# A memset ahead of the second of three loads in a 180-degree rotation

## The chip, the cores and the metric

The kernel runs on one core of one Trainium2 chip. The metric is device time in microseconds (us), taken from whole executions; the times before are the median of three. A profile is one more execution, recorded by the hardware profiler; its span goes from the first to the last instruction, so it is a little shorter than the device time. A core has five instruction queues that matter here by name: VectorE (DVE in the profile) does the copies, SyncE (SP) and ScalarE (ACT) issue transfers, GpSimd (POOL) sets four constants at the start, TensorE (PE) has no work. Transfers between the main memory (HBM) and the on-chip memory (SBUF, 128 partitions) run on 16 DMA engines, which all queues share.

## The reference

```python
def setup_inputs():
    batch, c, h, w = 32, 3, 256, 256
    return {"x": np.random.randn(batch, c, h, w).astype(np.float32)}

def reference(x: np.ndarray) -> np.ndarray:
    return np.rot90(x, k=2, axes=(-2, -1)).astype(np.float32)
```

Each of the 96 images of 256 x 256 numbers is turned by 180 degrees. As an image lies row after row, this is the same as writing its 65,536 numbers in reverse order. Nothing is calculated: 25.17 MB are read and 25.17 MB are written.

## The kernel before

The 96 images are cut into three groups of 32. In a group every image is cut into four quarters of E = 16384 numbers, so that a group fills a tile of 128 partitions (32 images x 4 quarters) with 16384 columns of float32: 64 KB a partition, 8.39 MB a tile. There are three such tiles, one for each group: `A`, `Bt` (called Bt in the profile, B by its tag) and `Ct`. A fourth, `T`, has J = 2048 columns and holds what is set aside in a swap. No tile is used twice for different groups, so the loads wait for nothing.

To reverse an image, the numbers inside each quarter are reversed by VectorE in the tile, and the four quarters of an image change places when the tile is stored: the output's access pattern has `::-1` over the four.

- `load` (line 54) issues one transfer for a whole tile. SyncE issues the loads of `A` and `Ct` (lines 69 and 71), ScalarE that of `Bt` (line 70). This is all that ScalarE does.
- `swap` (line 61) exchanges one block of columns at the front with its mirror block at the back, both reversed, by three copies on VectorE: the back block reversed into `T`, the front block reversed into the back, `T` into the front. `copy` (line 52) keeps these copies in the order of the program.
- `turn` (line 73) does this for a range of the front half in blocks of at most 2048 columns.
- `store` (line 57) issues one transfer from a tile to the output, on SyncE.

The order on VectorE is written out by hand: three blocks of `A`, a first piece of `Bt` (MID = 1008 columns), the last block of `A`, the rest of `Bt`, then `Ct`: 39 copies in all. SyncE issues, after its two loads, a first store of `A` (LEAD = 256 columns), the rest of `A`, then `Bt` and `Ct`, each when VectorE is done with it. Semaphore waits are put in by the framework from which instruction writes and which reads a tile: a load waits for an earlier instruction that writes the same columns, a copy for the load of its tile, a store for the copies.

Of the kernel before, what the change touches and what calls it, by code (L numbers as in the profile page):

```python
# [2 lines left out]

os.environ.setdefault("NEURON_RT_ULTRASERVER_MODE", "4")

# [4 lines left out]


@with_exitstack
def kernel(
    ctx: ExitStack,
    tc: tile.TileContext,
    x: bass.AP,
    out: bass.AP,
):

    nc = tc.nc
    P = 128

    B, C, H, W = x.shape
    L = H * W
    G = 32
    E = L // 4
    J = E // 8

    x4 = x.rearrange("b c h w -> (b c) (h w)").rearrange(
        "(g n) (s e) -> g (n s) e", n=G, s=4)
    o4 = out.rearrange("b c h w -> (b c) (h w)").rearrange(
        "(g n) (s e) -> g n s e", n=G, s=4)  # L40

    pool = ctx.enter_context(tc.tile_pool(name="slots", bufs=1))
    A = pool.tile([P, E], x.dtype, tag="A")
    Bt = pool.tile([P, E], x.dtype, tag="B")
    Ct = pool.tile([P, E], x.dtype, tag="C")
    T = pool.tile([P, J], x.dtype, tag="T")

    def back(t, lo, hi):
        return t[:, hi - 1:(lo - 1 if lo else None):-1]

    def copy(dst, src):
        tc.keep_in_program_order(nc.vector.tensor_copy(out=dst, in_=src))  # L52

    def load(t, g, lo, hi, queue=nc.sync):
        return queue.dma_start(out=t[:, lo:hi], in_=x4[g][:, lo:hi])

    def store(t, g, lo, hi):
        return nc.sync.dma_start(
            out=o4[g][:, ::-1, lo:hi], in_=t[:, lo:hi])

    def swap(t, lo, w):
        hi = E - lo - w
        copy(T[:, 0:w], back(t, hi, hi + w))
        copy(t[:, hi:hi + w], back(t, lo, lo + w))
        copy(t[:, lo:lo + w], T[:, 0:w])

    MID = 1008
    LEAD = 256
    load(A, 0, 0, E)
    load(Bt, 1, 0, E, nc.scalar)  # L70
    load(Ct, 2, 0, E)

    def turn(t, lo, hi):
        while lo < hi:
            w = min(J, hi - lo)
            swap(t, lo, w)
            lo += w

    half = E // 2
    turn(A, 0, half - J)  # L80
    store(A, 0, 0, LEAD)
    turn(Bt, 0, MID)
    turn(A, half - J, half)
    store(A, 0, LEAD, E)
    turn(Bt, MID, half)
    store(Bt, 1, 0, E)
    turn(Ct, 0, half)
    store(Ct, 2, 0, E)


# [1 line left out]
_INS = ['x']  # L92
_OUTS = [((32, 3, 256, 256), 'float32')]


# [23 lines left out]
```

## Time and profile before

| | us |
|---|---|
| device time, median of 3 runs (lowest to highest) | 122.11 (122.02 to 122.21) |
| span of the profiled execution, first to last instruction | 120.5 |
| VectorE busy in it, 39 copies | 44.7 |
| VectorE's wait for A's load, before its first copy | 42.0 |
| first copy starts, last copy ends | 41.99, 87.95 |
| SyncE's last issue, the store of Ct, starts | 87.98 |

The profiled execution has no device time of its own beside its span; the median stands for the runs without the profiler.

Section 1 of the profile's page gives the busy time of each engine, section 5 the costliest groups of instructions. A group's line reads: line of the kernel, engine, operation, what is written and read, with shape and type; how often; busy time in us and the mean of one in ns; and the idle time of the engine just before, with what ended it:

```profile
DVE 44.7 (37%) x39; POOL 0.2 (0%) x4
...
L52 DVE COPY T<-A 128x2048 f32<-128x2048 f32 x4 | 4.9, 1227 | 42.1 <-DMA A<-in_x_dram 42.0
```

A copy of 2048 columns takes 1227 ns, and VectorE's only long wait is the one for the first load.

In the DMA part, q1 is the queue of SyncE and q10 that of ScalarE; a line gives packets, MB and the time that the packets took as a share of 16 engines' span. A line of the DMA issues gives what was moved, the queue that issued it (SPq, ACTq), how often, KB where known, and the us from issue to landing. A line of the waits gives who waited, for what, and us in total, times, longest. A line of the timeline gives start and duration in us. A DMA packet here is one partition's row of a tile.

### The profile page before, as it was taken

The numbers are of one execution on the slowest core, as the hardware profiler recorded it, in microseconds if no ns is written. First come the engines' busy times: TensorE is split into PE (matmuls) and PEld (weight loads), VectorE is DVE, ScalarE is ACT, GpSimd is POOL, SyncE is SP. The second block draws the span as 40 slices with busy tenths as digits, with TensorE's granted clock in tenths as the row PEclk, the third lists the DMA queues.
The fourth block names the chain that finished last, engine by engine and source line by source line (L and its number), as shares of the span: only waits on it lengthen the run. The fifth ranks groups of instructions, "written<-read, shape, count | busy, mean of one in ns | idle before, by whom it ended". The sixth has DMA issues, their size and how long they took to land.

```text
span 120.5 us, 96 instructions
## 1 busy us (share of the span) xinstructions
DVE 44.7 (37%) x39; POOL 0.2 (0%) x4
## 2 busy tenths in 40 slices
DVE  0000000000000099999999999999910000000000
POOL 0000000000000000000000000000000000000000
DMA  9888988898889888988999977988898889888980
GB/s 348 348 348 370 674 348 348 370 652 370 348 370 652 370 348 348 674 370 348 348 386 599 428 343 343 664 369 348 348 674 370 348 348 674 370 348 348 674 370 0
DMA packets 1008, 50.33 MB, mean 418 GB/s; under 512 B 112, under 2 KB 240, under 8 KB 240
## 3 DMA queue, kind: packets, MB, share of 16 engines
q1 hardware_dynamic: 864, 41.94, 81.3%
q10 hardware_dynamic: 144, 8.39, 16.1%
HBM read 25.17 MB, written 25.17 MB: 418 GB/s over the span
## 4 chain that ended last, share of the span: by engine, by line
DVE 37%; DMA 34%; issue 1%
DMA A<-in_x_dram 34%; DVE T L52 12%; DVE Bt L52 9%; DVE A L52 8%; DVE Ct L52 8%
## 5 line engine op out<-in xcount | busy, mean ns | idle before, releaser
L52 DVE COPY T<-A 128x2048 f32<-128x2048 f32 x4 | 4.9, 1227 | 42.1 <-DMA A<-in_x_dram 42.0
L52 DVE COPY Bt<-T 128x2048 f32<-128x2048 f32 (+2 forms) x5 | 5.1, 1014 | 0.2
L52 DVE COPY T<-Bt 128x2048 f32<-128x2048 f32 (+2 forms) x5 | 5.1, 1014 | 0.2
L52 DVE COPY Bt<-Bt 128x2048 f32<-128x2048 f32 (+2 forms) x5 | 5.1, 1013 | 0.2
L52 DVE COPY T<-Ct 128x2048 f32<-128x2048 f32 x4 | 4.9, 1228 | 0.1
L52 DVE COPY A<-T 128x2048 f32<-128x2048 f32 x4 | 4.9, 1227 | 0.1
L52 DVE COPY Ct<-T 128x2048 f32<-128x2048 f32 x4 | 4.9, 1227 | 0.1
L52 DVE COPY Ct<-Ct 128x2048 f32<-128x2048 f32 x4 | 4.9, 1227 | 0.1
L52 DVE COPY A<-A 128x2048 f32<-128x2048 f32 x4 | 4.9, 1226 | 0.1
L103 POOL MEMSET const-bfloat16-1.0<- 128x1 bf16 x1 | 0.1, 101 | 0.0
L103 POOL MEMSET const-uint8-127<- 128x1 uint8 x1 | 0.1, 101 | 0.0
L103 POOL MEMSET const-float32-0.0<- 128x1 f32 x1 | 0.1, 98 | 0.2 <-issue 0.2
L103 POOL MEMSET const-float32-1.0<- 128x1 f32 x1 | 0.1, 98 | 0.0
## 6 DMA issues: line engine op xcount, KB each, us to landing
out_dram<-A SPq DMA_DIRECT2D x1, 8064.0 KB, 21.9
out_dram<-A SPq DMA_DIRECT2D x1, 128.0 KB, 16.3
Bt<-in_x_dram ACTq DMA_DIRECT2D x1, 41.4
A<-in_x_dram SPq DMA_DIRECT2D x1, 41.2
Ct<-in_x_dram SPq DMA_DIRECT2D x1, 60.5
out_dram<-Bt SPq DMA_DIRECT2D x1, 27.6
out_dram<-Ct SPq DMA_DIRECT2D x1, 31.8
```

The costliest lines, as they stand in the source:

```text
L52: tc.keep_in_program_order(nc.vector.tensor_copy(out=dst, in_=src))
L103: nc = _bacc.Bacc("TRN2", target_bir_lowering=False, num_devices=1)
```

## The change

Before the load of `Bt` is issued, VectorE sets the first 256 columns of `Bt` to zero. The load writes the same columns afterwards, so it waits on VectorE's semaphore for the memset; what is computed stays the same. The loads of `A` and `Ct` touch other tiles and have no wait, as before. The empty lines that are taken out of the function move the line numbers by eight, no instruction.

```diff
     load(A, 0, 0, E)
+    nc.vector.memset(Bt[:, 0:256], 0.0)
     load(Bt, 1, 0, E, nc.scalar)
     load(Ct, 2, 0, E)
```

In the changed program VectorE's queue holds the memset and then the same 39 copies in the same order; ScalarE's queue holds Bt's load with a wait on VectorE's semaphore; SyncE's queue holds the same six transfers in the same order.

## The prediction

> **What bounds the kernel now.** I read the waits of SyncE's queue first, then the table of DMA issues and the DMA part of the page, and only then the chain of waits, because that chain misleads here: it follows VectorE's copies (37% of the span) and one load (34%), its last piece is the copy that ends at 87.95 us, and the 32 us after that are not in it. The end is set by DMA. The waits of SyncE's queue say so:
>
> ```profile
> SPq L114 <- DMA out_dram<-Ct: 19.3, 1, 19.3
> SPq L114 <- DMA out_dram<-Bt: 11.8, 1, 11.8
> ```
>
> After its last issue SyncE only waits for the stores of Bt (11.8 us) and of Ct (another 19.3 us). The page's DMA part shows why they are late:
>
> ```profile
> DMA  9888988898889888988999977988898889888980
> q1 hardware_dynamic: 864, 41.94, 81.3%
> q10 hardware_dynamic: 144, 8.39, 16.1%
> HBM read 25.17 MB, written 25.17 MB: 418 GB/s over the span
> ```
>
> The two queues together keep the 16 DMA engines busy for 81.3 + 16.1 = 97.4% of the span, and no slice but the last is empty. q10 is ScalarE's queue, which carries Bt's load alone (8.39 MB); q1 is SyncE's, which carries the other 41.94 MB in its order: A, Ct, then four stores. The issues:
>
> ```profile
> out_dram<-A SPq DMA_DIRECT2D x1, 8064.0 KB, 21.9
> Bt<-in_x_dram ACTq DMA_DIRECT2D x1, 41.4
> A<-in_x_dram SPq DMA_DIRECT2D x1, 41.2
> Ct<-in_x_dram SPq DMA_DIRECT2D x1, 60.5
> out_dram<-Bt SPq DMA_DIRECT2D x1, 27.6
> out_dram<-Ct SPq DMA_DIRECT2D x1, 31.8
> ```
>
> Added to their issue times: A lands at 41.96, Bt at 42.1, Ct at 61.7; the stores at 81.1, 100.4 and 119.7. These are six transfers of 8.39 MB at about 19.3 to 21 us each, with nothing between them. VectorE has room everywhere. It issues A's main store at 59.28, and the ring is free for stores at 60.9 to 61.4; Bt's store is issued at 72.84 and its turn comes 8.3 us later; Ct's is issued at 87.98 and its turn comes 12.4 us later.
>
> Which transfer goes first was read from the start, first the instructions and then the packets of 0 to 4.7 us and of 4.7 to 7.1 us:
>
> ```profile
> 0.73 0.38 ACTq L55 DMA_DIRECT2D Bt<-in_x_dram  x1
> 0.73 0.39 SPq L55 DMA_DIRECT2D A<-in_x_dram  x1
> 1.18 0.43 SPq L55 DMA_DIRECT2D Ct<-in_x_dram  x1
> ```
>
> ```profile
> DMA packets 16, 1.05 MB, mean 223 GB/s; under 512 B 0, under 2 KB 0, under 8 KB 0
> q1 hardware_dynamic: 16, 1.05, 65.0%
> ```
>
> ```profile
> DMA packets 16, 1.05 MB, mean 437 GB/s; under 512 B 0, under 2 KB 0, under 8 KB 0
> q10 hardware_dynamic: 16, 1.05, 100.8%
> ```
>
> A and Bt are issued in the same instant, yet all 16 engines carry a packet of A first (64 KB, one partition's row) and then all 16 one of Bt. The packet records go on so, A, Bt, A, Bt, eight of each per engine, then eight of Ct. Bt is ready long before its first turn. A packet takes 2.42 us in the steady state; the first ones of A take 2.70 to 3.37 us (mean 3.05), start between 1.76 and 2.48 us and end between 4.75 and 5.38 (mean 5.04).
>
> The end follows from one engine, the one whose first packet ends last. By its packet records: issue at 0.73; first packet 1.43 us after that, at 2.16; 3.22 for it, to 5.38; 56.02 for its other 23 load packets, to 61.40; 0.35 for the small first store of A; 57.65 for 24 store packets, to 119.40; 0.34 to the last landing at 119.74; 0.79 for the closing barrier. Sum 120.53, the span of 120.5. The gap of 0.63 us between the first and the last engine at 5 us (5.38 - 4.75) is still 0.55 us at the end (119.40 - 118.85). The median of the runs, 122.11, lies 1.6 us above this span; I hold that constant and apply differences to the median.
>
> **The change part by part.** It adds one memset on VectorE, one wait on ScalarE's queue, and removes nothing.
>
> *The memset.* The trace has none on VectorE. Nearest rows: VectorE's copies take 685 ns for 1008 columns and 1227 for 2048, so (1227 - 685)/1040 = 0.52 ns a column and 0.16 us fixed; 256 columns would be 0.16 + 0.13 = 0.29 us. Below, GpSimd's one-column memsets take 0.10 us; above, a whole 1008-column copy takes 0.69. I take 0.29, the row of the same engine scaled to the size. On VectorE it costs nothing: the engine sits idle for 41.99 us before its first copy. Without that cover its 0.29 us would lie ahead of all 39 copies; A's store, with 1.6 us of room less about 1 us for a start of packets, would still just be in time. The Trainium skill ("VectorE: DVE Perf Modes", Zero memsets can be issued as uint32) states one cycle per element; at the 0.96 GHz of its specifications that is an estimate of 0.27 us, and no run here shows it.
>
> *The wait on ScalarE.* Only Bt's load stands on that queue, so nothing is queued behind it. Bt's issue moves from 0.73 to 0.73 + 0.29 + 0.02 (the step seen from a copy's end at 45.75 to the store it releases at 45.77) = 1.04 us; with the bounds 0.85 to 1.44. First packets of A came 1.03 to 1.75 us after their issue, so Bt is ready by 2.07 to 2.79, at worst 3.19. Its turn comes at 4.75 on the earliest engine, at least 1.56 us later. So I expect the order A, Bt, A, Bt to stay. If this cover were gone, the engine would take A's second packet, not idle: q1 alone holds 16 packets per engine. The late Bt itself costs nothing.
>
> *What A gains.* SyncE's issue of A is no longer made in the same 0.4 us as ScalarE's issue of Bt; for some 0.31 us it is alone. The trace of before doesn't show how A's first packets come when nothing else is being issued. Lower bound: nothing, the spread of 0.73 us over the engines is A's own. Upper bound: every engine ends its first packet where the best now does, a gain of 5.38 - 4.75 = 0.63 us on the engine that sets the end. I take the slowest moving to the mean, 5.38 - 5.04 = 0.34 us; halving the spread of the starts gives about the same, 0.73/2 = 0.36. A loss has its own mechanism, below. As the engines go from packet to packet without idling, this 0.34 us should arrive unshortened at the end: A's landing, VectorE's copies and the stores all move with it. SyncE's own issues of A and Ct aren't moved; Bt's issue, at 1.04, comes to lie over Ct's at 1.18, and both are needed only later (4.75 and about 41 us).
>
> The row says A's first packets have a spread that a competitor could have caused. The Trainium skill speaks against that gain ("DMA: Bandwidth & Descriptors", Issuing engines are not separate DMA queues): transfers of all issuing engines share the same 16 DMA engines, and issuing from several saves only the sequencer's time. By that rule a shifted issue changes nothing and the sum is 122.11; by the row it is 121.77. The packets' alternation agrees with the rule's first half, and no run yet shows a lone issue.
>
> **Sum.** 0 (memset, hidden) + 0 (Bt's wait, hidden) - 0.34 (A's first packets) = -0.34: span 120.19, median 121.77.
>
> **The rivals.** *Nothing arrives.* The spread is how one load is handed to 16 engines, whoever else issues; Bt waits 0.31 us within a slack of 1.56 or more. For it: Bt had to wait for its turn anyway, and SyncE's issue of Ct, alone on its side at 1.18, took 0.43 us, no less than A's 0.39 beside ScalarE's. Against it: the first packets differ by 0.7 us both in start and in duration, while later ones are all 2.42. Time 122.11. Here belongs also the variant that Bt misses its first turn and the order is A, A, Bt: A would land 2.42 us sooner, VectorE would start sooner, and the stores would still stand in q1 behind Ct's load until 61 us.
>
> *The collision moves onto A's first packets: slower.* Bt's and Ct's issues now fall together at 1.04 to 1.6 us, so that two loads' descriptors, not one's, are handed out while A's first packets run (1.76 to 5.38). If their extra 0.63 us (3.05 - 2.42) is what Ct's descriptors cost them now, twice as many cost another 0.63: 122.74, and half of it 122.42. It decides as soon as these packets' mean is more than 0.24 us over 3.05. Against it: at 72.84 and 87.98, when Bt's and Ct's stores are issued, the packets under way keep their 2.38 to 2.42 us.
>
> *The change doesn't do what it says.* The load could be let go without the wait; but the changed program has the wait on VectorE's semaphore at this load. It would again be 122.11, and counts with the first rival.
>
> **How the numbers follow.** A measurement of this kernel can tell about 0.2%, 0.24 us, from no change. The gain through A's first packets, at 0.24 to 0.63 us, has 0.47; nothing arrives, with smaller gains, 0.35; the collision, 0.18. So faster 0.47, same 0.35, slower 0.18. The time is that of the likeliest, 121.77; its own range is 121.48 to 121.87. The range I give runs from the upper bound of the gain, 122.11 - 0.63 = 121.48, rounded out to 121.45, up to the collision at half its price, 122.42, rounded out to 122.45.
>
> **What would show it.** Right: the issue of Bt near 1.04; all 16 first packets still A's and the next 16 Bt's; A's first packets starting within 0.4 us of each other and all ended by about 5.05; A landing near 41.6; Ct's store landing near 119.4. Nothing arrives: starts still spread over 0.7 us, landing at 119.7. Collision: first packets over 3.3 us in the mean. The prediction would be wrong altogether if the steady packets' 2.42 us changed, or if a gap opened between load and store packets at 61 us.

## The result, and the profile after

The changed kernel takes 122.83 us (median of 4 runs, 122.78 to 122.89); the kernel before, run beside it, 122.06 us (121.82 to 122.21). The ratio is 1.0069, with a 95% interval of 1.0055 to 1.0083: 0.8 us slower, against a forecast of 0.34 us faster, and outside the range that was given. The span of the profiled execution grew from 120.5 to 121.1 us.

First the timeline of the changed kernel's start (start and duration in us, then the instruction):

```profile
0.73 0.39 SPq L47 DMA_DIRECT2D A<-in_x_dram  x1
0.85 0.27 DVE L62 MEMSET Bt<- 128x256 f32 x1 [0.85 <-PEq L96]
1.15 0.39 ACTq L47 DMA_DIRECT2D Bt<-in_x_dram  x1
1.18 0.42 SPq L47 DMA_DIRECT2D Ct<-in_x_dram  x1
39.50 1.23 DVE L44 COPY T<-A 128x2048 f32<-128x2048 f32 x1 [38.38 <-DMA A<-in_x_dram]
```

The memset takes 0.27 us and Bt's load is issued at 1.15, 0.42 us later than before. Yet VectorE's first copy starts at 39.50 instead of 41.99. The packets of 4.7 to 7.1 us say why; here they belong to SyncE's queue, where before they were ScalarE's:

```profile
DMA packets 16, 1.05 MB, mean 437 GB/s; under 512 B 0, under 2 KB 0, under 8 KB 0
q1 hardware_dynamic: 16, 1.05, 100.8%
```

Every engine carries a second packet of A before the first of Bt. The order is A, A, Bt, A, Bt and so on, with two of Bt at the end, and A lands one packet sooner. That is followed by the copies and the stores, as the DMA issues of the changed kernel show:

```profile
out_dram<-A SPq DMA_DIRECT2D x1, 8064.0 KB, 24.9
...
A<-in_x_dram SPq DMA_DIRECT2D x1, 38.8
Bt<-in_x_dram ACTq DMA_DIRECT2D x1, 43.1
Ct<-in_x_dram SPq DMA_DIRECT2D x1, 61.1
out_dram<-Bt SPq DMA_DIRECT2D x1, 30.7
out_dram<-Ct SPq DMA_DIRECT2D x1, 34.8
```

A's main store is issued at 56.79 instead of 59.28, 2.49 us sooner, but lands only 24.9 us later, at 81.7 instead of 81.1. Ct's load, issued at 1.18 in both, lands 61.1 instead of 60.5 us after its issue. So the time was lost before the stores began, inside the loads. VectorE, 2.49 us ahead of its old times, gained nothing for the end: of the waits of SyncE's queue, the one for Ct's store is as long as before, and the one for Bt's store has taken up the time that VectorE is ahead.

```profile
SPq L107 <- DMA out_dram<-Ct: 19.3, 1, 19.3
SPq L107 <- DMA out_dram<-Bt: 14.9, 1, 14.9
```

The place shows when the packets are counted in narrow windows. Between 57.8 and 59.8 us each of the 16 engines starts exactly one packet, the eighth and last of Ct. The last figure of the line is the time that the window's packets took as a share of 16 engines in 2 us, so that it gives their mean length: first the kernel before,

```profile
q1 hardware_dynamic: 16, 1.05, 138.4%
```

which is 2 x 1.384 = 2.77 us, and then the changed kernel,

```profile
q1 hardware_dynamic: 16, 1.05, 167.7%
```

which is 3.35 us. The steady packet takes 2.42 us in both. On the engine that sets the end, the packet records give the whole difference: first packet ended at 5.29 us instead of 5.38 (-0.09); its other load packets take 56.69 us instead of 56.02, and of these 0.67 us the last packet alone has 0.72 (3.51 instead of 2.80); the small store and the 24 store packets take 0.35 and 57.65 us in both. It ends at 119.98 instead of 119.40, and the last landing is at 120.32 instead of 119.74.

In both kernels a store stands in the queue behind that last load packet. In the kernel before it is only the small first store of A; in the changed one A's main store stands there too, issued at 56.79 us, before the packet starts at 58.03 to 58.46.

### The profile page after: what moved, and what is told of

Same layout as the page of the kernel before. It is cut to its first block, busy times and chain, and to the rows that moved or that the text cites. A ratio compares the mean times of both kernels' runs of the same rounds, so it can differ in the third digit from the quotient of the medians.

```text
span 121.1 us, 97 instructions
## 1 busy us (share of the span) xinstructions
DVE 44.9 (37%) x40; POOL 0.2 (0%) x4
## 4 chain that ended last, share of the span: by engine, by line
DVE 37%; DMA 32%; issue 1%
DMA A<-in_x_dram 32%; DVE T L44 12%; DVE Bt L44 8%; DVE A L44 8%; DVE Ct L44 8%
## 6 DMA issues: line engine op xcount, KB each, us to landing
out_dram<-A SPq DMA_DIRECT2D x1, 8064.0 KB, 24.9
Ct<-in_x_dram SPq DMA_DIRECT2D x1, 61.1
```

## Experiments

Three theories at first. S: a main store that stands ready behind the last load packets stretches them. V: VectorE, which is ahead and on Bt instead of A at 58 to 61 us, disturbs the last load. O: the order A, A, Bt, or the late Bt, costs by itself. All edits are to the changed kernel unless another is named. Each kernel was timed beside the kernel before, whose medians were 121.98 to 122.02 us.

**hold_store.** ScalarE copies columns of A onto themselves before the store; values stay the same, and only the store's issue moves.

```diff
     turn(A, half - J, half)
+    hold = half - 2560
+    nc.scalar.copy(out=A[:, hold:half], in_=A[:, hold:half])
     store(A, 0, LEAD, E)
```

> The changed kernel, with A's main store alone held back: ScalarE first copies 2560 columns of A onto themselves, some 2.3 us, so the store is issued near 59.2 us instead of 56.8; VectorE's order and times stay. Theory S (a main store that stands ready behind the last load packets stretches Ct's last packet, 3.36 us in the mean after against 2.77 before): that packet falls back to 2.7 to 2.9 us and the time to 121.9 to 122.2. Rival V (VectorE, now 2.49 us ahead and on Bt instead of A at 58 to 61 us, disturbs the last load): packet near 3.36 us, time 122.8. Rival O (the order A, A, Bt or the late Bt costs): 122.8 as well.

Its timeline, and then its packets of 57.8 to 59.8 us:

```profile
56.77 2.33 ACT L78 COPY A<-A 128x2560 f32<-128x2560 f32 x1 [15.96 <-DVE A L44]
56.77 1.23 DVE L44 COPY T<-Bt 128x2048 f32<-128x2048 f32 x1
58.03 1.23 DVE L44 COPY Bt<-Bt 128x2048 f32<-128x2048 f32 x1
59.12 0.55 SPq L50 DMA_DIRECT2D out_dram<-A  x1
```

```profile
q1 hardware_dynamic: 16, 1.05, 122.5%
```

VectorE's copies stand where they stood in the changed kernel, the order of packets is A, A, Bt, and the store alone is 2.33 us later. The last packet falls to 2.45 us, and the time to 122.02 us, ratio 1.0001 (0.9988 to 1.0015). V and O fall with this one run.

**before_mid0.** The reverse: the kernel before, without memset, with an earlier store.

```diff
-    MID = 1008
+    MID = 0
```

> The kernel before, without a memset, with MID = 0: A's last block no longer waits for a piece of Bt, and A's main store is issued near 57.1 us instead of 59.28; the order of packets stays A, Bt, A, Bt. Theory S: Ct's last packet near 3.3 us, time 122.6 to 122.8, as slow as the changed kernel without its change. Rival O (order or late Bt): 122.1. Rival V (VectorE on Bt at 58 to 61 us): 122.6 to 122.8.

```profile
57.14 0.55 SPq L50 DMA_DIRECT2D out_dram<-A  x1
```

```profile
q1 hardware_dynamic: 16, 1.05, 162.2%
```

The order is A, Bt, A, Bt, the store is issued at 57.14, and the last packet takes 3.24 us: 122.88 us, ratio 1.0068 (1.0046 to 1.0090). The changed kernel's loss, 1.0069, appears without the change and without its order of packets. MID = 0 also brings VectorE to Bt sooner, which V would blame too, but that cause is out by hold_store; what is left is the earlier store.

**after_mid2272.** MID = 2272 gives the changed kernel a later store by moving copies of Bt ahead.

> The changed kernel with MID = 2272: VectorE turns more of Bt ahead of A's last block, and A's main store is issued near 59.3 us as in the kernel before. Theory S and rival V: 121.9 to 122.2, Ct's last packet 2.7 to 2.9 us. Rival O: 122.8.

Store at 59.40, last packet 2.71 us, 122.06 us, ratio 0.9995 (0.9980 to 1.0010): as S has it, and against O.

**memset_1col.** How far must Bt be late for the order to turn?

```diff
-    nc.vector.memset(Bt[:, 0:256], 0.0)
+    nc.vector.memset(Bt[:, 0:1], 0.0)
```

> The changed kernel with a memset of 1 column: Bt's load is issued near 0.98 us instead of 1.15. If the engine picks its second packet soon after the first (its descriptors taken ahead), the order is A, A, Bt on the engines where Bt comes too late and A, Bt on the others: A lands between 39.5 and 42, and by theory S the time follows the issue of A's main store: 122.8 if it is issued at 56.8, 122.1 if at 59.3. If the order is A, Bt on all engines, 122.1 or, by the gain that was forecast, 121.8.

```profile
0.80 0.06 DVE L62 MEMSET Bt<- 128x1 f32 x1 [0.80 <-PEq L96]
0.89 0.37 ACTq L47 DMA_DIRECT2D Bt<-in_x_dram  x1
```

Issued at 0.89 us, Bt still gets its turn on all 16 engines; the store is issued at 59.26, the last packet takes 2.51 us, and the time is 122.05 us, ratio 1.0003 (0.9988 to 1.0017). The forecast gain doesn't come: the first packets of A still start over 0.84 us and end at 5.02 us in the mean, against 5.04 before.

The next question was what the price depends on.

**after_mid0.** MID = 0 in the changed kernel: the store comes earlier still.

> The changed kernel with MID = 0: A's main store is issued near 54.6 us, 2.2 us earlier still, so that its descriptors have been handed out before Ct's seventh packet ends. Theory H (a price paid once, where the first store packet stands ready behind the last load packet): only Ct's last packet is stretched, 3.3 to 3.4 us, time 122.7 to 122.9 as after. Rival C (a ready store competes with the loads for as long as it waits): Ct's seventh packet is stretched too, time 123.2 or more. Rival G (handing out the store's descriptors while a load packet runs is what stretches it): the stretch moves to Ct's seventh packet and the last falls back to 2.42 to 2.5.

Store at 54.78. Ct's seventh packet takes 2.43 us, its last 3.54: 122.94 us, ratio 1.0083 (1.0070 to 1.0096). The price is paid at the last packet, and waiting 2 us longer adds at most some 0.1 us, which the intervals don't tell from nothing. C and G fall.

**after_one_store.** Without the small first store:

```diff
-    store(A, 0, 0, LEAD)
...
-    store(A, 0, LEAD, E)
+    store(A, 0, 0, E)
```

> The changed kernel with A stored in one transfer, issued near 56.8 us, without the first small store of 256 columns. Theory H: the price does not need the small store: Ct's last packet 3.2 to 3.4 us; the small packets' 0.35 us are gone from between and stand in the store's own packets, time 122.7 to 122.9. Rival L (the small packets together with the ready main store make the price): Ct's last packet 2.42 to 2.8 us, time 122.0 to 122.3.

Last packet 3.53 us, 122.91 us, ratio 1.0081 (1.0069 to 1.0094). The small store isn't needed for the price; L falls.

**before_mid1600.** The store later than before, at 60.38 us.

> The kernel before with MID = 1600: A's main store is issued near 60.2 us, 0.93 us later than before. Theory H: Ct's last packet falls to 2.42 to 2.5 us; if the store's first packet still comes in time, 121.7 to 121.9, which beats both kernels; if a gap opens behind the small store (descriptors near 61.2 to 61.9, wanted from 61.0), the gain is given back: 122.0 to 122.4.

The last packet takes 2.70 us, not the 2.5 expected, and a gap of up to 0.30 us opens behind the small store; the main store's packets start at 61.64 us in the mean, against 61.40. Time 122.31 us, ratio 1.0026 (1.0014 to 1.0038): too late costs as well.

**store_on_act.** The store on ScalarE's queue.

```diff
-    def store(t, g, lo, hi):
-        return nc.sync.dma_start(
+    def store(t, g, lo, hi, queue=nc.sync):
+        return queue.dma_start(
...
-    store(A, 0, LEAD, E)
+    store(A, 0, LEAD, E, nc.scalar)
```

> The changed kernel with A's main store issued by ScalarE, on the other ring, near 56.8 us: its packets take turns with Ct's last ones instead of standing behind them. Theory H: the price is paid at each change from load to store, one or two times: time 122.8 to 123.4. Rival R (the price belongs to one ring, where the next packet is taken ahead): no packet is stretched, 121.7 to 122.1.

Issued at 56.88; the last packet of Ct takes 3.44 us again, and A's first main packet follows it within 0.2 us on every engine. 123.09 us, ratio 1.0088 (1.0075 to 1.0101). The price doesn't belong to one ring. This fits what the Trainium skill says ("DMA: Bandwidth & Descriptors", Issuing engines are not separate DMA queues), that the queues share the same engines.

**hold_1200 and hold_1900.** The hold of the first experiment, shorter (1200 and 1900 columns instead of 2560), to find when the store counts as ready.

> The changed kernel with ScalarE's hold of 1200 columns, some 1.1 us: A's main store is issued near 57.95 us, so that its descriptors (about 1 us later) come shortly after Ct's last packet has started at 57.9 to 58.5. Theory P (the engine takes its next packet ahead when the present one starts, and the price falls due only if the store's packet is there by then): Ct's last packet 2.42 to 2.8 us, time 122.0 to 122.2. Rival W (the price grows with how long the store stands ready inside that packet, some 2 of 2.9 us): last packet near 3.1, time 122.4 to 122.6.

> The same with a hold of 1900 columns, some 1.75 us: the store is issued near 58.55 us. Theory P: as with the kernel before, 122.0 to 122.2. Rival W: last packet near 2.9, time 122.2 to 122.4.

Store issued at 58.07 and, in the profiled execution, at 59.03 (VectorE was some 0.45 us late there, so the runs without the profiler may lie nearer the 58.55 expected). Last packets 2.88 and 2.57 us; times 122.59 us, ratio 1.0055 (1.0034 to 1.0075), and 121.94 us, ratio 1.0002 (0.9989 to 1.0015). Neither theory has both: P misses the first, whose last packet started at 57.85 to 58.50, before the store's descriptors can have come (1.03 us or more after the issue, going by A's load); W's times fit the first and miss the second, and its packet lengths miss both. These two profiles lie at the edge of their runs: hold_1200's execution took 122.32 us, the lowest of six, hold_1900's 122.68, the highest of twelve. The price falls away within about 1 us of delay.

**mid1600_lead1024.** Bridging the gap of before_mid1600 with a larger first store.

```diff
-    MID = 1008
-    LEAD = 256
+    MID = 1600
+    LEAD = 1024
```

> The kernel before with MID = 1600 (A's main store issued near 60.4 us, too late to stand ready) and a first store of 1024 instead of 256 columns, which bridges the gap (8 packets of 4 KB an engine, about 1.2 us instead of 0.37). If only large store packets that stand ready cost anything: no gap, Ct's last packet 2.42 to 2.8, time 121.7 to 122.0. If the first store's packets of 4 KB cost as much as the main store's: last packet 3.2 to 3.5 us, time 122.6 to 122.9.

```profile
q1 hardware_dynamic: 16, 1.05, 173.0%
```

The last packet takes 3.46 us though the main store is issued only at 60.21: 122.91 us, ratio 1.0074 (1.0056 to 1.0092). Eight ready store packets of 4 KB on an engine cost as much as packets of 63 KB. Eight of 1 KB stand ready in the kernel before and in hold_store, where the last packet is 0.03 (2.45) and 0.35 us (2.77) over the steady one, and in before_mid1600, where the main store came too late to stand ready, 0.28 us (2.70).

**ct_tail.** The last load packets made small.

```diff
-    load(Ct, 2, 0, E)
+    load(Ct, 2, 0, E - 1024)
+    load(Ct, 2, E - 1024, E)
```

> The changed kernel with Ct's load cut in two, the last 1024 columns as a transfer of its own, so that the last load packets are 8 of 4 KB an engine instead of one of 64 KB. Theory H (a fixed price at the step from loads to a ready store): some 0.6 to 0.9 us are lost around the small packets, time 122.7 to 123.0. Rival Q (the packet before the store runs slower for its whole length, so the price is in proportion to it): 0.9/16 of it is left, time 122.0 to 122.3.

The eight small load packets of an engine take 0.28 us in the mean, but not evenly. Two windows in which only small load packets start, of 59.92 to 60.92 and of 61.25 to 61.65 us, show it:

```profile
q1 hardware_dynamic: 28, 0.11, 78.7%
```

```profile
q1 hardware_dynamic: 39, 0.16, 96.9%
```

The first line is 0.787 x 16 engines x 1 us over 28 packets, a mean of 0.45 us; the second, in the same way, is 0.16 us, the pace of the 4 KB store packets of mid1600_lead1024 (0.159). So the first small packets are slow, and those directly ahead of the stores are not. Over the eight, 8 x (0.282 - 0.159) = 0.98 us are lost, about as much as on one packet of 64 KB. Time 123.35 us, ratio 1.0109 (1.0088 to 1.0129), slower than either theory had it. Q's share of 0.9/16 is far too small. A roughly fixed sum fits, but it is paid some way ahead of the stores, within the last 2 to 3 us of the loads, and not on the packet that stands next to them. No run has the small tail without a ready store, so whether a part of this loss comes from the step to small load packets stays open.

Together, for the kernels that keep the transfers of the kernel before, in order of the main store's issue. Issue and last packet (the mean of the 16 engines) are from the one profiled execution, the median is from all runs:

| kernel | order | store issued, us | last load packet, us | median, us |
|---|---|---|---|---|
| after_mid0 | A, A, Bt | 54.78 | 3.54 | 122.94 |
| changed kernel | A, A, Bt | 56.79 | 3.35 | 122.83 |
| before_mid0 | A, Bt | 57.14 | 3.24 | 122.88 |
| hold_1200 | A, A, Bt | 58.07 | 2.88 | 122.59 |
| hold_1900 | A, A, Bt | 59.03 | 2.57 | 121.94 |
| hold_store | A, A, Bt | 59.12 | 2.45 | 122.02 |
| memset_1col | A, Bt | 59.26 | 2.51 | 122.05 |
| kernel before | A, Bt | 59.28 | 2.77 | 121.98 to 122.06 |
| after_mid2272 | A, A, Bt | 59.40 | 2.71 | 122.06 |
| before_mid1600 | A, Bt | 60.38 | 2.70 | 122.31 |

The time goes by the store's issue, whatever the order of the first packets. The best place lies between 59.0 and 59.4 us, perhaps from 58.6 on if hold_1900's other runs issue where it was expected, and the kernel before stands in it. No version beat it.

What happens inside a DMA engine when a ready store follows a load, for instance whether it begins to read the store's data while the load is still being written, stays open: the runs show when the price is paid and how much, not by what.

## Why the prediction was wrong

*What bounds the kernel.* Right. The end is set by the DMA queues without idling, and VectorE's 2.49 us came to nothing. The sum along one engine held too, save for its last load packet. The start carries to the end: in the profiled execution of hold_1900 one engine's first packet ended at 5.73 us, against 4.71 to 5.38 on the others, and this engine's stores ended last, at 119.74 against 118.54 to 119.06.

*The memset.* Taken at 0.29 us, measured 0.27. Bt's issue was put at 1.04 and came at 1.15, inside the bounds; the memset itself started at 0.85, later than I had set it.

*"So I expect the order A, Bt, A, Bt to stay."* Wrong. I counted the slack up to the second packet's start at 4.75 us. The engines choose it about two microseconds or more ahead: Bt issued at 0.89 got its turn on all engines, issued at 1.15 on none, though its descriptors, if they took the 1.03 to 1.75 us that A's took, were there by 2.18 to 2.90 us. If Bt's lag on an engine is the same as A's, issued at 0.73, the choice falls between 0.16 and 0.42 us after the first packet's start; that is an estimate, and no record shows the choice itself.

*The gain of 0.34 us.* It did not come. A's first packets have a mean of 3.02 us against 3.05, start over 0.65 us against 0.73, and end at 5.04 us in the mean in both kernels; on the slowest engine they end between 5.26 and 5.73 us from kernel to kernel, with no pattern that I could tie to an edit. The rule that I set against the row, that separate issue saves only issue time, was the right side for these packets; the 122.11 that I drew from it, with a shifted issue changing nothing, was not.

*The step that failed.* The sum had two terms wrong: the gain of 0.34 us, which measured as nothing, and, the larger miss, the 0 for Bt's wait ("hidden"). Bt lost its first turn, and the price of that is in the first rival. There I named the order A, A, Bt with its landing 2.42 us sooner, and priced it at nothing, since "the stores would still stand in q1 behind Ct's load until 61 us". Standing there is what costs. The runs show in its place a loss of 0.8 to 0.9 us (medians of 122.83 to 122.94 against 121.98 to 122.06) for a main store that is issued 2 us or more sooner, before the last load packet starts. A sign to see beforehand was in the trace of before: Ct's last packet took 2.77 us; I used the sum of the 23 load packets, 56.02 us, without asking why it exceeds 23 x 2.42 = 55.66.

*The rival on the slower side*, a collision of issues on A's first packets, was not the cause: those packets did not get longer. Its lower price, 122.42, lay closer to the result, but for a reason that fell.

## What to carry to other kernels

In a kernel bound by DMA, an earlier landing need not be a gain: look at what it makes ready sooner, and at which transfer that will stand behind. Where loads turn into stores, price the step itself, by the length of the last load packets against the steady ones, and set the issue of the first large store so that it arrives just as the loads end; here issues at 59.0 to 59.4 us did well, 58.07 and 60.38 did not. A wait placed on a queue can act through the order of packets long before the data is needed.

## What the runs showed of the hardware

- The step from loads to stores has a price of its own: 0.8 to 1.1 us an engine over the steady 2.42 us packet when store packets of 4 KB or more stand ready behind the last load at or near its start (3.24 to 3.54 us; in ct_tail 0.98 us over eight small packets, all of it on the earlier ones), 0.46 us when the main store is issued at 58.07 us, early in the last packet (2.88), and 0.03 to 0.35 us when it is issued at 59.0 to 59.4 us (2.45 to 2.77).
- The turn between two queues goes by single packets of 64 KB: A, Bt, A, Bt. The Trainium skill ("DMA: Bandwidth & Descriptors", Queues, rings and completion order) speaks of packets of typically 9 to 17 descriptors before an engine turns to the next queue; here, where an engine carries 8 rows of a load, it turned after each row.
- The next packet is chosen well ahead: 0.26 us in the issue of a load (0.89 against 1.15) moved its first packet from the second place to the third, by a packet of 2.42 us, though the second place came only at 4.7 us or later.
